# The second half's norm in five steps between the next sub-layer's weight tiles, and the old x fetched in two parts

## The chip, the cores and the metric

The kernel runs on 1 core of one Trainium2 chip. Its time is the device time of one execution in microseconds (us); the median of several executions counts, and lower is better. The engines of the core run side by side and wait for each other on semaphores: TensorE (PE for matmuls, PEld for their weight loads), VectorE (DVE), ScalarE (ACT), GpSimd (POOL) and the queue SP, which issues most of the DMAs. Each engine takes its instructions in the order in which they stand in its program.

## The reference, cut to what matters

The reference is one inference step through two layers of a decoder, for 512 prompt tokens and 64 sample tokens (8 sequences of 8) together, with a model width of 1024 and everything in float32. Each layer has three sub-layers: a SwiGLU feed-forward network (FFN), a token mixer (layer 0: a Mamba-2 state-space mixer, layer 1: sliding-window attention), and another FFN.

```python
for i in range(DEPTH):                                   # 2 layers
    mod = (cs @ ada_w[i] + ada_b[i]).reshape(bsz, 1, N_SUB, 3, D_MODEL)
    hin = modulated_norm(x, norm_pre[i, 0], mod[:, :, 0])
    f = swiglu(hin, ffn_w_in[i, 0], ffn_w_out[i, 0])
    x = x + FFN_RES * mod[:, :, 0, 2] * rms_norm(f, norm_post[i, 0])
    hin = modulated_norm(x, norm_pre[i, 1], mod[:, :, 1])
    o, ... = mixer(hin, ...)
    x = x + mod[:, :, 1, 2] * rms_norm(o, norm_post[i, 1])
    hin = modulated_norm(x, norm_pre[i, 2], mod[:, :, 2])
    f = swiglu(hin, ffn_w_in[i, 1], ffn_w_out[i, 1])
    x = x + FFN_RES * mod[:, :, 2, 2] * rms_norm(f, norm_post[i, 2])
```

Here `modulated_norm(x, g, m)` is `rms_norm(x, g) * (1 + m[:, :, 1]) + m[:, :, 0]`, and `swiglu` is `(silu(g) * u) @ w_out` with `g, u` the two halves of `h @ w_in`. Between two sub-layers, then, x gets the normed and gated output f of the one before, and a second norm of the new x makes the next input, hin.

## The kernel before

**Layout.** All activations are held with the model width on the 128 partitions, in 8 tiles (index k or o), and the 576 tokens along the free dimension. The tokens are worked on in two parts, which this document calls halves: half 0 is 256 prompt tokens, half 1 the other 256 prompt tokens and the 64 sample tokens (320 columns). Every weight and activation is split into a high part and a low part, so a product of a 128x128 weight tile is three matmuls (low weight x high activation, high x low, high x high), and a tile of 128 outputs over 1024 inputs is 8 x 3 = 24 matmuls per half. `load_w` fetches a weight tile by DMA into `raw` (two buffers), ScalarE casts the high part (L469, `whi` or, where extra buffers are borrowed, `wx`), and VectorE subtracts it to get the low part (L472).

**A boundary between sub-layers** is an object of `Boundary`. There are six; the last one writes the output. The five others go like this:

1. The last weights of the sub-layer are loaded in `run_out`. Before them, `open` fetches the old x from the DRAM copy `x_dram` in three DMAs (L94): x[0] (half 0, 1 MB), x[1] (the prompt tokens of half 1, 1 MB) and x[2] (the sample tokens, 256 KB).
2. `stat` gathers, for each output tile, the squares of f and, for half 0 on GpSimd (L335), the product of the old x[0] with f; for half 1 the products with x[1] and x[2] are matmuls (`gram`, L343).
3. `sums` turns them into two scales per token. They are broadcast over the partitions by matmuls into `rb` (L255): b1 for f, b2 for the new x.
4. `update(h)` adds the scaled f to x (L414, L415) and writes the normed `hin` of that half (L436 on VectorE, L438 on ScalarE, L439 on VectorE), two k at a time; for half 1 it does the sample tokens first (L407, L409, then L445 to L449). `update(0)` runs while `run_out` still works on half 1.
5. The next sub-layer begins in `run_in`: it takes the weights that `run_out` has already begun to load, loads the rest of the first 8 (an FFN) or 6 (a mixer), calls `update(1)`, and then does all these weight tiles on half 0 and after that all of them on half 1.

**What consumes the first weight tiles.** Each product goes to one of 4 PSUM buffers `g` (L501), and its `use` function frees that buffer. In an FFN the tiles alternate: a gate tile is read by ScalarE (`silu`, L724, into one of 3 `sil` buffers), an up tile by VectorE (L729, which frees the PSUM buffer), ScalarE (L730) and VectorE (L731, which frees the `sil` buffer). In the state-space mixer the first tile gives the time steps (L1100, ScalarE), and the next five are convolutions: a copy out of PSUM (L849, ScalarE, 2 buffers `xpt`), a first tap on ScalarE (L860), three taps on VectorE for half 0 (L863), a tanh (L869) and a last product (L870, VectorE); `acc`, which two of these share, has 2 buffers. After all six, `dt_path` computes the decays in one chain, mostly on VectorE. In attention the first six tiles are only copied out by ScalarE.

**What sets the order on an engine.** The program text gives priorities, not an order: a scheduler runs the program through a model of the chip and lets each engine take, among the instructions that are ready in the model's time, the one that stands first in the text. The order so found is fixed in the program. A few orders are pinned by hand with `behind`: `place(1, base)` puts the matmuls of the sums and of the two broadcasts of half 1 (`PL[1] = (25, 52, 64)`) behind the 26th, 53rd and 65th matmul of the next sub-layer.

Of the kernel before, what the change touches and what calls it, by code (L numbers as in the profile page):

```python
# [58 lines left out]
def body(ctx: ExitStack, tc: tile.TileContext, A, O):  # L59
# [28 lines left out]

    XO = ((0, 2048), (2048, 2048), (4096, 512))

    def x_copy(d, x, store):
        for t, (o, n) in zip(x, XO):
            a, b = d[:, o:o + n], t.rearrange("p k n -> p (k n)")
            nc.sync.dma_start(a if store else b, b if store else a)  # L94

    x = x_alloc()
# [39 lines left out]
    x_dram = dram.tile([128, 8 * T], F32, name="x_dram")  # L136
# [159 lines left out]
    class Boundary:  # L296
# [5 lines left out]
            self.end = (l, s) == (1, 2)  # L302
            self.marks = [{}, {}]

        def open(self):
            l, s = self.l, self.s
            state["xp_cm"] = tc.tile_pool(name=f"xpool{l}{s}", bufs=1, side="right", reuse_waits="tile")
            state["xp"] = state["xp_cm"].__enter__()
            x_cur[:] = x_alloc()
            x_copy(x_dram if l or s else A["xT"], x_cur, False)  # L310
            self.cms = [tc.tile_pool(name=f"{n}{l}{s}", bufs=1, side="right", reuse_waits="tile") for n in ("upd", "stats")]
            self.pool, pool = (cm.__enter__() for cm in self.cms)
            self.spool = pool
            mod_gate(l, s, self.mv)
            self.ns = 1 if self.end else 2
            self.gram = [None, None]
            self.acc = [pool.tile([128, 3 - h, n], F32, tag=f"st{h}", name=f"st{h}") for h, (_, n) in enumerate(HALF)]
            if not self.end:
                self.nmv = mod_vecs(*((l, s + 1) if s < 2 else (l + 1, 0)))
# [75 lines left out]
            self.cms.pop().__exit__(None, None, None)  # L395

        def update(self, h):
            f, b1 = self.f, self.b1
            if not self.end:
                b2 = self.b2  # L400
                if h == 0:
                    self.hin = hin_alloc()
            if self.end:
                return self.finish(h)
            if h == 1:
                ts = self.pool.tile([128, 8, 64], F32, tag="ts", name="ts", bufs=1)
                V.tensor_tensor(out=ts, in0=f[1][:, :, 256:320], in1=b1[:, 256:320].unsqueeze(1).to_broadcast([128, 8, 64]),  # L407
                                op=ALU.mult)
                V.tensor_tensor(out=x_cur[2], in0=x_cur[2], in1=ts, op=ALU.add)  # L409
                if not self.end:  # L410
                    norm_sample(self.pool, self.nmv, b2, self.hin)
            for kk in range(0, 8, 2):
                fs, xs = f[h][:, kk:kk + 2, 0:256], x_cur[h][:, kk:kk + 2, :]
                V.tensor_tensor(out=fs, in0=fs, in1=b1[:, 0:256].unsqueeze(1).to_broadcast([128, 2, 256]), op=ALU.mult)  # L414
                V.tensor_tensor(out=xs, in0=xs, in1=fs, op=ALU.add)  # L415
                if not self.end:
                    norm_prompt(self.pool, self.nmv, b2, self.hin, h, (kk, kk + 1))

        def finish(self, h):

# [60 lines left out]
    def gemm(w, acts, n, w0=0):  # L481

        return gemms([w], acts, n, w0)[0]
# [21 lines left out]
    def hin_acts(hin, h):  # L505
        return [(hin[h][:, 0, k, :], hin[h][:, 1, k, :]) for k in range(8)]
# [10 lines left out]
    def run_in(hin, items, first, ex, pend, between=None, pre=()):  # L517

        bd = last.pop() if first and last else None
        base = len(mms)  # L520
        ws = [bd.nextw[i] if bd and i < len(bd.nextw) else pre[i][0] if i < len(pre) else
              load_w(src, 1024, ex if i >= WR else None)
              for i, (src, _) in enumerate(items[:first])]
        if bd:
            bd.update(1)
            bd.close()
        for h in (0, 1):
            if between and h:
                between()
            for i, (w, (_, use)) in enumerate(zip(ws, items)):  # L530
                if h == 0 and i < len(pre):
                    use(h, gemm_part(w, hin_acts(hin, h), HALF[h][1], range(4, 8), pre[i][1]))
                else:
                    use(h, gemm(w, hin_acts(hin, h), HALF[h][1]))
            if bd and h == 0:
                bd.place(1, base)
        for src, use in items[first:]:
            w = load_w(src, 1024)
            for h in (0, 1):
                use(h, gemm(w, hin_acts(hin, h), HALF[h][1]))  # L540
            pend.step()
# [11 lines left out]
    def run_out(loads, acts, f, first, bd=None, r=0, ex=None, bias=None):  # L553


        def one(w, w0, o, h):
            t0, n = HALF[h]
            p = gemm(w, acts(h), n, w0)
            fs = f[h][:, o, :]
            if first:  # L560
                if bias is None:
                    S.copy(fs, p)
                else:
                    S.activation(out=fs, in_=p, func=AF.Identity, bias=bias[:, o:o + 1])
            else:
                V.tensor_tensor(out=fs, in0=p, in1=fs, op=ALU.add)  # L566
            if bd:
                bd.stat(o, h)

        nl = len(loads) - r  # L570
        for src, n, os_ in loads[:nl]:
            w = load_w(src, n)
            for o, w0 in os_:
                for h in (0, 1):
                    one(w, w0, o, h)
        if r:
            ws = [load_w(src, n, ex if i >= WR else None) for i, (src, n, _) in enumerate(loads[nl:])]
            todo = [(w, w0, o) for w, (_, _, os_) in zip(ws, loads[nl:]) for o, w0 in os_]
            for a in todo:
                one(*a, 0)  # L580
            base = len(mms)
            for a in todo[:B1]:
                one(*a, 1)
            bd.sums(0)
            for a in todo[B1:B2]:
                one(*a, 1)
            bd.update(0)
            for a in todo[B2:]:
                one(*a, 1)
            bd.place(0, base)  # L590
            bd.nextw = [load_w(src, 1024) for src in first_srcs(bd)]
            bd.sums(1)
            bd.close()
            if bd.end:
                bd.finish(1)
                bd.close()
            else:
                last.append(bd)
# [109 lines left out]
    def ffn(l, s, hin, f, pend, bd):  # L708
        si = 0 if s == 0 else 1
        sub = lambda name: tc.tile_pool(name=f"{name}{l}{s}", bufs=1, reuse_waits="tile")  # L710
        with sub("mid") as mp:
# [50 lines left out]
            pend.flush()  # L762
            ada_cm.__exit__(None, None, None)
            with sub("tail") as tp:
                bd.open()
                run_out(loads, halves(mids), f, False, bd, RF, borrow(tp, "wf", 2 * (RF - WR), mk * 128))


    def ssd(l, hin, f, pend, bd):
        with ExitStack() as cx:  # L770
# [336 lines left out]
            d, items = proj_items(0)  # L1107
# [57 lines left out]
            R2cm.__exit__(None, None, None)  # L1165
            Rcm.__exit__(None, None, None)
            with tc.tile_pool(name="ssdo", bufs=1, reuse_waits="tile") as ap[0]:
                bd.open()
                run_out(out_loads(3), yn_acts(yn), f, False, bd, 4)


# [514 lines left out]
```

## Time and profile before

| | |
|---|---|
| median of 3 runs | 2581.92 us (2581.41 to 2588.04) |
| the profiled execution | 2593.07 us, of which 2591.0 us from its first instruction to its last |
| mean granted TensorE clock | 0.977 of full |
| busy share: PE, PEld, DVE, ACT, POOL | 96%, 89%, 70%, 44%, 8% |
| DMA | 331 MB, 128 GB/s over the span |

The profiled execution lies 11.15 us above the median. Matmuls overlap each other, so the busy share of PE is not a share of its peak; what PE loses is seen in the gaps and in the granted clock, stretch by stretch. Matmul counts of a stretch include those that reach over its edges.

### The profile page before, as it was taken

To read this page: it belongs to the slowest core of one execution; us is meant where nothing else is said; L and a number is where in the kernel's file an instruction comes from. 1 tells how busy PE (TensorE), PEld (TensorE's weight loads), DVE (VectorE), ACT (ScalarE), POOL (GpSimd) and SP (SyncE) were. 2 spreads that over 40 slices of the span, in tenths; PEclk is the share of its full clock that TensorE was granted. 3 is DMA by queue.
4 is the path that set the end of the run, shared out by engine and by line. 5 is a ranking of instruction groups with operands and counts; after the bars stand their busy time and mean duration, and the time that the engine had idled before them with its cause. 6 is when DMAs were issued, how large, how long until landed. Compare 5 with 4: busy or idle time off the path is not lost.

```text
span 2591.0 us, 45688 instructions
## 1 busy us (share of the span) xinstructions
PE 2493.8 (96%) x18247; PEld 2309.2 (89%) x18247; DVE 1804.0 (70%) x3415; ACT 1152.3 (44%) x2396; POOL 202.8 (8%) x338
## 2 busy tenths in 40 slices
PE   6999999989999999999999999999999998999997
PEld 5999998877989878899999999999899788999997
DVE  5576766887768686667767757675766756577685
ACT  4343434554645454334424534342454664343343
POOL 1000000123131312000000100000010001000001
PEclk8999999999999999899999999999999998999998
DMA  7344534244444342344333343443436123233222
GB/s 261 106 167 135 191 134 167 94 117 130 122 131 107 131 115 107 120 138 127 122 135 120 121 139 107 167 177 126 168 124 202 34 70 107 94 101 103 91 94 110
DMA packets 119499, 331.04 MB, mean 128 GB/s; under 512 B 17903, under 2 KB 39903, under 8 KB 108671
## 3 DMA queue, kind: packets, MB, share of 16 engines
q1 hardware_dynamic: 100535, 245.46, 29.3%
q10 hardware_dynamic: 18752, 82.68, 9.3%
q8 instruction: 143, 2.34, 0.4%
q14 instruction: 69, 0.57, 0.1%
HBM read 301.63 MB, written 29.67 MB: 128 GB/s over the span
## 4 chain that ended last, share of the span: by engine, by line
PE 80%; DVE 8%; DMA 4%; ACT 3%; issue 3%; POOL 1%; SPq 0%; DVEq 0%; ACTq 0%; POOLq 0%
PE g L501 40%; PE g L673 29%; PE adaps L164 2%; DMA w<-scr_a 1%; PE gram L343 1%; DVE wlo L472 1%; DVE acc L863 1%; DMA raw<-in_w_out 1%; PE po L1298 1%; DVE hin L439 1%; PE py L947 1%; PE ssq L234 1%; DVE pn L436 1%; PE rb L255 1%; DMA x<-x_dram 1%
## 5 line engine op out<-in xcount | busy, mean ns | idle before, releaser
L501 PE MATMUL g<-hin,whi 128*128 128x320 f32 (+1 forms) x2528 | 533.4, 304 | 1.8 <-DVE hin L439 1.8
L501 PE MATMUL g<-mid,whi 128*128 128x320 f32 (+1 forms) x2432 | 489.3, 296 | 0.0
L673 PE MATMUL g<-hin,whi 128*128 128x288 f32 x2176 | 436.2, 294 | 0.0
L501 PEld LDWEIGHTS g<-hin,whi 128*128 128x128 f32 x2528 | 418.6, 194 | 10.3 <-issue 6.6
L501 PE MATMUL g<-hin,wlo 128*128 128x320 f32 (+1 forms) x1264 | 388.1, 309 | 16.1 <-ACT sil L724 7.0
L501 PEld LDWEIGHTS g<-mid,whi 128*128 128x128 f32 x2432 | 390.7, 188 | 1.1
L501 PE MATMUL g<-mid,wlo 128*128 128x256 f32 (+1 forms) x1216 | 359.8, 297 | 2.4 <-ACT mid L685 2.2
L673 PEld LDWEIGHTS g<-hin,whi 128*128 128x128 f32 x2176 | 349.1, 188 | 0.0
L673 PE MATMUL g<-tcmb,whi 128*128 128x288 f32 x1632 | 327.2, 294 | 0.0
L673 PE MATMUL g<-hin,wlo 128*128 128x288 f32 x1088 | 324.2, 298 | 0.0
L469 ACT CAST whi<-raw 128x1024 fp32r<-128x1024 f32 (+2 forms) x209 | 188.0, 900 | 236.3 <-PE g L501 162.5
L472 DVE TENSOR_TENSOR wlo<-raw,whi 128x1024 fp32r<-128x1024 f32 (+3 forms) x209 | 216.4, 1038 | 85.7 <-ACT whi L469 84.7
L501 PEld LDWEIGHTS g<-hin,wlo 128*128 128x128 f32 x1264 | 244.3, 194 | 33.7 <-issue 11.0
L673 PEld LDWEIGHTS g<-tcmb,whi 128*128 128x128 f32 x1632 | 262.5, 189 | 0.0
L673 PE MATMUL g<-tcmb,wlo 128*128 128x288 f32 x816 | 245.5, 301 | 0.0
L501 PEld LDWEIGHTS g<-mid,wlo 128*128 128x128 f32 x1216 | 228.6, 188 | 7.1 <-ACT mid L685 4.6
L652 ACT CAST whi<-scmb 128x512 fp32r<-128x512 f32 (+1 forms) x204 | 154.3, 760 | 160.8 <-PE g L673 83.5
L673 PEld LDWEIGHTS g<-hin,wlo 128*128 128x128 f32 x1088 | 204.1, 188 | 23.9 <-issue 23.9
L566 DVE TENSOR_TENSOR f<-g,f 128x256 f32<-128x256 f32 (+1 forms) x240 | 108.6, 455 | 143.4 <-PE g L501 142.2
L648 DVE TENSOR_TENSOR wlo<-scmb,whi 128x512 fp32r<-128x512 f32 (+1 forms) x204 | 175.6, 863 | 36.1 <-ACT whi L652 35.2
L673 PEld LDWEIGHTS g<-tcmb,wlo 128*128 128x128 f32 x816 | 153.3, 188 | 25.1 <-DVE ur L648 19.7
L652 ACT CAST whi<-raw 128x512 fp32r<-128x512 f32 x136 | 84.7, 623 | 166.2 <-PE g L673 98.4
(299 smaller groups left out, 3898.9 us busy)
## 6 DMA issues: line engine op xcount, KB each, us to landing
adaw<-in_ada_w ACTq DMA_DIRECT2D x56, 1024.0 KB, 5.4
raw<-in_w_in SPq DMA_DIRECT2D x108, 512.0 KB, 3.5
rawu<-in_w_in SPq DMA_DIRECT2D x68, 512.0 KB, 4.5
raw<-in_w_out SPq DMA_DIRECT2D x64, 384.0 KB, 3.1
raw<-in_w_out SPq DMA_DIRECT2D x64, 320.0 KB, 3.0
raw<-in_w_ssm SPq DMA_DIRECT2D x40, 512.0 KB, 3.5
x_dram<-x SPq DMA_DIRECT2D x10, 1024.0 KB, 3.9
x<-x_dram SPq DMA_DIRECT2D x10, 1024.0 KB, 6.3
```

The costliest lines, as they stand in the source:

```text
L164: PE.matmul(out=pt[32 * j:32 * j + 32, :w], lhsT=cs[:, k, :], rhs=aw[:, j * w:j * w + w], start=(k == 0), stop=(k == 7))
L234: ins = PE.matmul(out=ps[:, c0 + i:c0 + i + 1], lhsT=acc[:, o:o + 128], rhs=ones[:, 0:1], start=True, stop=True)
L255: ins = PE.matmul(out=r[:, c:e], lhsT=mul(y[:, i:i + 1], [128, 128]), rhs=ident[:, 128 - (e - c):128], start=True, stop=True)
L343: ins = PE.matmul(out=out, lhsT=a, rhs=b, start=(o == i == 0), stop=(o == 7), skip_group_check=True)
L436: V.scalar_tensor_tensor(out=tm, in0=x_cur[h][:, k, :], scalar=mv["gs"][:, k, 0:1], in1=r[:, :256], op0=ALU.mult, op1=ALU.mult)
L469: S.copy(hi[:, :n], raw[:, :n])
L472: i = (V if early and c < PSP else eng or V).tensor_tensor(out=lo[:, c:e], in0=raw[:, c:e], in1=hi[:, c:e].bitcast(F32), op=ALU.subtract)
L501: mms.append(PE.matmul(out=p[:, :n], lhsT=wt[:, a:b], rhs=at, start=(k == j == 0), stop=(j == 2 and k == K - 1)))
L566: V.tensor_tensor(out=fs, in0=p, in1=fs, op=ALU.add)
L648: e.tensor_tensor(out=out, in0=a, in1=b, op=op)
L652: S.copy(w[0][:, c:c + n], src)
L673: mms.append(PE.matmul(out=p, lhsT=wt[:, o], rhs=x, start=(first and k == j == 0), stop=(k == 3 and j == 2), skip_group_check=True))
```

## The change

`update` becomes a generator, `updates`, of five steps for half 1: the sample tokens, then k = 0 and 1, 2 and 3, 4 and 5, 6 and 7. `run_in` no longer does `update(1)` ahead of its products: it does one step after each of the first weight tiles on half 0 has been used, and closes the boundary's pool after the last of them. So a tile's `use` now stands in the text ahead of the steps that follow it. The instructions of the norm and of the `use` functions themselves are the same, and so are the pinned places.

Besides, `open(False)` fetches only x[0], in the four FFN sub-layers and in the state-space mixer; the DMAs of x[1] and x[2] stand in the text after the loads of the last weights in `run_out` (`bd.rest()`). Attention calls `open()` and keeps all three together.

```diff
-    def x_copy(d, x, store):
-        for t, (o, n) in zip(x, XO):
+    def x_copy(d, x, store, parts=(0, 1, 2)):
+        for t, (o, n) in ((x[i], XO[i]) for i in parts):
             a, b = d[:, o:o + n], t.rearrange("p k n -> p (k n)")
             nc.sync.dma_start(a if store else b, b if store else a)
...
+        def rest(self):
+
+            if self.more:
+                x_copy(*self.more, False, (1, 2))
+            self.more = None
+
-        def open(self):
+        def open(self, rest=True):
...
-            x_copy(x_dram if l or s else A["xT"], x_cur, False)
+            self.more = (x_dram if l or s else A["xT"], x_cur)
+            x_copy(*self.more, False, (0,))
+            if rest:
+                self.rest()
...
         def update(self, h):
+            for _ in self.updates(h):
+                pass
+
+        def updates(self, h):
...
                 if not self.end:
                     norm_sample(self.pool, self.nmv, b2, self.hin)
+                yield
             for kk in range(0, 8, 2):
...
                 if not self.end:
                     norm_prompt(self.pool, self.nmv, b2, self.hin, h, (kk, kk + 1))
+                yield
...
-        if bd:
-            bd.update(1)
-            bd.close()
+        steps = bd.updates(1) if bd else iter(())
         for h in (0, 1):
...
                     use(h, gemm(w, hin_acts(hin, h), HALF[h][1]))
+                next(steps, None)
             if bd and h == 0:
+                for _ in steps:
+                    pass
+                bd.close()
                 bd.place(1, base)
...
             ws = [load_w(src, n, ex if i >= WR else None) for i, (src, n, _) in enumerate(loads[nl:])]
+            bd.rest()
...
-                bd.open()
+                bd.open(False)
                 run_out(loads, halves(mids), f, False, bd, RF, borrow(tp, "wf", 2 * (RF - WR), mk * 128))
...
-                bd.open()
+                bd.open(False)
                 run_out(out_loads(3), yn_acts(yn), f, False, bd, 4)
```

## Rows read from the trace of the kernel before

**Rows 1.** The page, part 4: the chain that ended last, by engine.
```profile
PE 80%; DVE 8%; DMA 4%; ACT 3%; issue 3%; POOL 1%; SPq 0%; DVEq 0%; ACTq 0%; POOLq 0%
```

**Rows 2.** PE's timeline, starts of half 1 at three FFN entries.
```profile
1079.41 0.64 PE L501 MATMUL g<-hin,wlo 128*128 128x320 f32 x1 [3.26 <-ACT sil L724]
...
1508.80 2.97 PE L501 MATMUL g<-hin,wx 128*128 128x256 f32 x24
1515.47 0.63 PE L501 MATMUL g<-hin,wlo 128*128 128x320 f32 x1 [3.70 <-ACT sil L724]
...
2188.31 5.49 PE L501 MATMUL g<-hin,wx 128*128 128x256 f32 x24 [4.07 <-DVE sil L729]
```

**Rows 3.** Windows: length, busy of PE, PEld, DVE, ACT, POOL, PEclk, DMA, GB/s.
```profile
1515.00:1520.00 5.00, 4.53 (x17) 4.53 (x18) 2.71 (x8) 1.49 (x5) 0.00 (x0) 0.50 0.28 110
1520.00:1525.00 5.00, 5.00 (x31) 5.00 (x30) 1.23 (x1) 1.38 (x2) 0.00 (x0) 0.85 0.00 0
```

**Rows 4.** VectorE's timeline, second FFN entry shown (1492 to 1518 us).
```profile
1494.68 0.69 DVE L407 TENSOR_TENSOR ts<-f,rb 128x512 f32<-128x512 f32 x1 [0.71 <-PE rb L255]
...
1514.51 0.42 DVE L731 TENSOR_TENSOR mid<-sil,mid 128x256 fp32r<-128x256 f32 x1
1514.84 0.87 DVE L439 SCALAR_TENSOR_TENSOR hin<-pn,modraw,hin 128x256 fp32r<-128x256 f32 x2
1515.64 1.07 DVE L729 TENSOR_TENSOR sil<-g,sil 128x256 f32<-128x256 f32 x3
```

**Rows 5.** VectorE's timeline, first and third FFN entry (from 1076 and 2168 us).
```profile
1078.79 0.86 DVE L439 SCALAR_TENSOR_TENSOR hin<-pn,modraw,hin 128x256 fp32r<-128x256 f32 x2
...
2173.45 0.69 DVE L446 TENSOR_TENSOR pns<-pns,rb 128x512 f32<-128x512 f32 x1 [2.58 <-PE rb L255]
...
2188.18 0.86 DVE L439 SCALAR_TENSOR_TENSOR hin<-pn,modraw,hin 128x256 fp32r<-128x256 f32 x2
```

**Rows 6.** Windows (columns as in rows 3): matmuls that wait for hin, twice.
```profile
505.00:510.00 5.00, 3.20 (x15) 1.96 (x13) 4.52 (x12) 2.52 (x7) 0.10 (x1) 1.00 0.51 210
1043.00:1047.00 4.00, 1.78 (x8) 1.18 (x8) 4.00 (x10) 1.04 (x3) 0.00 (x0) 1.00 0.16 66
1048.00:1057.00 9.00, 8.60 (x41) 8.59 (x41) 3.48 (x8) 2.93 (x5) 2.74 (x7) 0.50 0.49 160
```

**Rows 7.** VectorE's timeline, entry of the state-space mixer (488 to 511 us).
```profile
490.87 0.51 DVE L863 SCALAR_TENSOR_TENSOR acc<-xpt,c_convw,acc 128x256 f32<-128x256 f32 x1 [1.97 <-ACT acc L860]
...
507.60 0.47 DVE L863 SCALAR_TENSOR_TENSOR acc<-xpt,c_convw,acc 128x256 f32<-128x256 f32 x1
```

**Rows 8.** PE's timeline, the longest stall on `xpt`, state-space entry.
```profile
523.42 9.24 PE L501 MATMUL g<-hin,wx 128*128 128x320 f32 x48 [2.58 <-ACT xpt L849]
```

**Rows 9.** Windows (columns as in rows 3): state-space entry, attention entry.
```profile
490.00:560.00 70.00, 59.81 (x400) 55.30 (x400) 62.77 (x130) 36.29 (x83) 17.76 (x39) 0.95 0.44 121
1930.00:1965.00 35.00, 35.00 (x272) 34.32 (x272) 30.95 (x60) 15.40 (x32) 3.24 (x7) 1.00 0.50 176
```

**Rows 10.** SP's timeline at the end of the first FFN.
```profile
421.22 8.52 SPq L467 DMA_DIRECT2D raw<-in_w_out  x4
429.78 2.19 SPq L94 DMA_DIRECT2D x<-in_xT  x3
433.47 1.71 SPq L467 DMA_DIRECT2D raw<-in_w_out  x2
```

**Rows 11.** PE's timeline there: the last weights of half 0.
```profile
436.27 4.47 PE L501 MATMUL g<-mid,wx 128*128 128x256 f32 x36
444.33 6.95 PE L501 MATMUL g<-mid,wx 128*128 128x256 f32 x36 [3.59 <-DVE wx L472]
```

**Rows 12.** The chain of waits there, in order of time.
```profile
429.78 5.80 DMA x<-in_xT
```

**Rows 13.** The page, part 6: DMA issues, KB each, us to landing.
```profile
raw<-in_w_in SPq DMA_DIRECT2D x108, 512.0 KB, 3.5
...
raw<-in_w_out SPq DMA_DIRECT2D x64, 384.0 KB, 3.1
```

More of the change, by code (lines that the diff above doesn't have):

```diff
@@ L403, in update @@
             if self.end:
-                return self.finish(h)
+                self.finish(h)
+                return
             if h == 1:
```

## The prediction

> **What bounds the kernel now.** I read the chain that ended last first: PE holds 80% of it [rows 1], so the time is PE's, and a change pays only where PE waits or runs at the lower clock. I then looked along PE's timeline for gaps, at the six boundaries above all, because that is where both edits work. Three things stand out.
>
> At each of the three FFN entries that follow a boundary, PE stops for 3.26, 3.70 and 4.07 us around the turn from half 0 to half 1, and what ends the wait is a `use`: the silu of a gate tile (L724) twice, the product of an up tile (L729) once [rows 2]. The reader is to see in VectorE's timeline why. The norm of half 1 starts with L407 at 1494.68, and nearly every `use` of an up tile stands behind it: three L729 in a row come only at 1515.64, behind the last L439 [rows 4]. With up tiles unread, PSUM and `sil` buffers stay taken, and PE has nowhere to write. After the stop the granted clock is 0.50 in a window with 17 matmuls in 4.53 us of PE's time, and 0.85 in the next [rows 3]; 0.85 of 5 us is 1.5 us more at half clock, so some 6.0 us from 1515.47 run at 1.2 instead of 2.4 GHz.
>
> At the entry of the state-space mixer VectorE is the busy one, 62.77 of 70 us [rows 9]; PE waits there first for hin and later for `xpt` (2.58 us in its longest stall) [rows 6, 8]. At the attention entry PE is busy for all of 35 us at clock 1.00 [rows 9], so nothing is to be had.
>
> At the end of the first FFN PE stops for 3.59 us before the last two weight tiles of half 0, and those 36 matmuls then take 6.95 us where the 36 before took 4.47 [rows 11]. The other three FFN ends have the same stop, of 2.68 to 3.39 us. The fetch of x[0], 5.80 us, lies on the chain just before [rows 12].
>
> **The norm in steps: an FFN entry.** No instruction is added or removed; 30 VectorE instructions of the norm and the L729 and L731 of the up tiles change places. In the new text tile 1 (up) stands ahead of the second step and tile 3 (up) ahead of the fourth; tiles 5 and 7 stand behind all five. In the old order tile 1's L731 (1514.51) already ran ahead of the last L439 (1514.84) [rows 4], so only tile 3 puts something new ahead of the norm's end: one L729 and one L731, 1.07/3 = 0.36 us each [rows 4], 0.7 us together. In return tiles 1 and 3 free their PSUM and `sil` buffers early, and PE can go on until it lacks hin. What is late next is therefore the last pair of hin: PE needs it for the last 6 of the 24 matmuls of the first tile of half 1. A half-0 tile takes 2.97 us [rows 2], so by columns (320 for 256) I estimate a half-1 tile at 3.6 us and six matmuls at 0.9.
>
> - Second entry shown. Lost before: the stop of 3.70, and the clock: 6.0 us / 0.267 = 22 matmuls, each 4.53/17 - 3.6/24 = 0.117 us slower, 2.6 us. Together 6.3. After: half 0 ends at 1508.80 + 2.97 = 1511.77, an unhindered first tile would end 3.6 later at 1515.4; the last hin comes at 1514.84 + 0.87 + 0.7 = 1516.4, and with 0.9 the tile ends at 1517.3 [rows 2, 4]. Lost after: 1.9. Gain 4.4.
> - First entry, in the same way: 3.26 + 2.6 (taken over, since it restarts at the same place) = 5.9 before; last hin 1078.79 + 0.86 + 0.7, tile end 1081.3, against 1076.15 + 3.6 = 1079.8: 1.5 after [rows 2, 5]. Gain 4.4.
> - Third entry: here the stop falls before the last tile of half 0, whose 24 matmuls take 5.49 instead of 2.97 us [rows 2]: 4.07 + 2.5 = 6.6. VectorE sits idle for 2.58 us before L446 at 2173.45 [rows 5]; tile 1's two instructions fit into that. Last hin 2188.18 + 0.86 + 0.7 + 0.9 = 2190.6, unhindered end 2184.24 + 2.97 + 3.6 = 2190.8: nothing lost after. Gain 6.6.
>
> Together 15.4 us. Each has two ends: nothing, if the wait for hin takes the whole place of the old one, and all of what was lost (5.9, 6.3, 6.6, in sum 18.8). I stay with the worked values, because they follow instruction by instruction from the old order. The cover that this needs is that PE's first 18 matmuls of half 1 find their hin. A wait is added too: L729 of tile 3 waits for PE, with the fourth and fifth step queued behind it on VectorE and half 1 waiting for those. Where the fixed order puts it too early, that is at most one tile, 2.97 us [rows 2], per entry.
>
> **The norm in steps: the state-space entry.** Here each `use` costs VectorE four instructions (three L863, one L870), and tiles 1 to 4 stand ahead of the last step; of the first tile one L863 ran before the norm anyway, and its next came only at 507.60 [rows 7]. So up to 15 instructions of 0.47 us, 7 us, move ahead of the last hin, and half 1 with the time-step chain behind it starts that much later. In return the convolutions no longer pile up: the stall of 2.58 us [rows 8] and its like are theirs. VectorE's idle time between 490 and 560 us is 70 - 62.77 = 7.2 us [rows 9], and no more than that can be won while it is the bound. Between -7 and +7.2 I take 0. The attention entry, whose `use` functions need no VectorE and which has no gap, gets 0 too.
>
> **x in two parts.** The text of the old kernel has the three x DMAs ahead of all eight weight loads, and yet SP issued six of those first, then the three x, then the last two [rows 10]. The queue goes by readiness, then. x[1] and x[2] were issued by 429.78 + 2.19 = 431.97, and the next weight load not before 433.47, since its buffer has to be freed by VectorE. Moving x[1] and x[2] behind it in the text does not make that buffer free sooner; they should leave at the same moment as before, and the edit costs and gives nothing. If they did leave last, they would be covered: half 1 begins no sooner than 444.33 + 6.95 = 451.3 [rows 11]. What that would give: a 512 KB load lands in 3.5 us and one of 384 KB in 3.1 [rows 13], so 0.4 per 128 KB, and 1 MB alone at 3.5 + 1.6 = 5.1 against 5.80 [rows 12]: 0.7 us at each of four FFN ends, 2.8 us at the low end; at the high end the whole stop with its clock, 3.59 + 2.48 = 6.1 [rows 11], 24 us for four. The Trainium skill (DMA: Bandwidth & Descriptors, section on queues, rings and completion order) says that each DMA engine consumes the descriptors of one ring in ring order. By that rule x[1] and x[2], which stand behind x[0], never held it up, and the gain would be 0 even if they moved; the trace before has no x[0] fetched alone to show it.
>
> **The sum.** 15.4 + 0 + 0. The profiled execution took 2593.07 us, so it would take 2577.7; the median of the runs shown is 11.15 us lower, and the same gain taken from 2581.92 gives 2566.5.
>
> **Rivals.**
> - The clock falls all the same. Matmuls that dribble as hin arrives kept clock 1.00 from 505 to 510 us, with 3.20 us of PE busy in 5, but after 1043 to 1047, with 1.78 in 4, nine us ran at 0.50 [rows 6]. I expect 3.6 us of work in about 5, nearer the first. If it falls at all three entries, 2.6 each goes back: 2566.5 + 7.8 = 2574. The Trainium skill (TensorE: Matmul & The Clock Gate, "Loop structure matters more than you think") speaks for this rival: it calls a wait in front of every matmul the loop that goes cold.
> - x[1] and x[2] do leave behind the last weights: 2.8 to 24 us more, 2542 to 2564. Against it stands the order that SP shows [rows 10].
> - Slower, through the state-space entry: if each of tiles 1 to 4 holds the norm not for its instructions alone but for its whole way over ScalarE as well, it is 1.97 + 4 x 0.47 = 3.9 us per tile [rows 7], 15.5 for four, and a clock fall of 2.6 on top: 18 us late, and the decay chain with it. That is 2 to 3 us more than the FFN entries bring: 2585. It decides from 15.4 us; beyond 23 the kernel is slower by more than 0.3%. For it: VectorE is nearly full there. Against: the same convolutions are then out of the way later.
> - The scheduler's order hardly changes. It takes what is ready in the model's time; if the model sees the up tiles ready late, the norm still goes first: 2582. Against: tile 1's L729 and half of its work already slip ahead.
>
> **How the numbers follow.** A difference within 0.3% (7.7 us) can hardly be told from none here. Forecast 0.45 (own range 2559 to 2574), clock 0.17, x 0.12, state-space 0.14, no new order 0.12. The forecast, x and half of the clock case are faster, 0.66; the rest of the clock, no new order and nearly half of the state-space case are the same, 0.25; 0.09 slower. The range reaches from forecast plus the 7.2 of the state-space entry and part of the x case (2555) to the state-space rival's 2585.
>
> **What would show it.** Right: L729 of tile 3 ahead of the last L439 at the FFN entries; PE's stops of 3.26, 3.70 and 4.07 gone, with short ones on hin instead, at clock 1.00; SP with x, x, x before the last two weight loads, and the 3.59 us stop of the first FFN's end still there. Wrong: a window at 0.50 after those entries; a stop before half 1 at the state-space entry well above 7 us; x[1] issued after the last w_out load.

## The result, and the profile after

The changed kernel takes 2559.75 us (median of 6 executions, 2557.07 to 2561.28); the kernel before took 2587.35 us beside it (2581.41 to 2591.27). The ratio is 0.9894, with a 95% interval of 0.9879 to 0.991: 27.6 us less, where 15.4 were forecast. The profiled execution took 2559.38 us, with a span of 2557.2 us and a mean granted clock of 0.984 (before 2591.0 and 0.977).

The chain that ended last is still PE's (page, part 4, shares by engine; before [rows 1]):
```profile
PE 81%; DVE 8%; DMA 4%; ACT 4%; issue 2%; POOL 1%; SPq 0%; DVEq 0%; ACTq 0%; POOLq 0%
```

**The FFN entries.** PE's timeline after, at the first and second entry, answers [rows 2]. The lines of the kernel have shifted: L501 is now L517, the gate's silu L743, the up product L748, the last step of hin L455.
```profile
1075.18 0.42 PE L517 MATMUL g<-hin,wlo 128*128 128x320 f32 x1 [1.22 <-ACT hin L454]
...
1502.42 0.56 PE L517 MATMUL g<-hin,whi 128*128 128x320 f32 x2 [0.17 <-DVE hin L455]
```
The stops of 3.26, 3.70 and 4.07 us are gone. What is left waits for hin, 1.22 and 0.17 us, and at the third entry nothing. VectorE's timeline at the second entry answers [rows 4]:
```profile
1495.86 0.41 DVE L748 TENSOR_TENSOR sil<-g,sil 128x256 f32<-128x256 f32 x1
...
1503.47 0.41 DVE L748 TENSOR_TENSOR sil<-g,sil 128x256 f32<-128x256 f32 x1
1503.80 0.87 DVE L455 SCALAR_TENSOR_TENSOR hin<-pn,modraw,hin 128x256 fp32r<-128x256 f32 x2
```
The reader is to see two up products ahead of the last L455, where before three in a row came behind it (in both kernels one more, tile 1's, runs ahead of the whole norm). The first 10 us of half 1 at the three entries, in windows (columns as in [rows 3]: length, busy of PE, PEld, DVE, ACT, POOL, clock, DMA, GB/s):
```profile
1071.00:1081.00 10.00, 8.78 (x60) 8.51 (x59) 8.80 (x20) 4.74 (x11) 0.00 (x0) 1.00 0.27 107
1500.04:1510.04 10.00, 9.83 (x68) 9.56 (x67) 8.34 (x17) 5.31 (x10) 0.00 (x0) 1.00 0.31 114
2164.20:2174.20 10.00, 10.00 (x71) 10.00 (x70) 8.27 (x18) 5.21 (x10) 0.00 (x0) 1.00 0.26 107
```
The clock is 1.00 in all of them; [rows 3] had 0.50 and 0.85 at the second entry.

**The FFN ends.** SP's timeline at the end of the first FFN answers [rows 10]:
```profile
420.28 8.65 SPq L483 DMA_DIRECT2D raw<-in_w_out  x4
428.97 0.43 SPq L94 DMA_DIRECT2D x<-in_xT  x1
432.65 1.70 SPq L483 DMA_DIRECT2D raw<-in_w_out  x2
434.40 0.90 SPq L94 DMA_DIRECT2D x<-in_xT  x2
```
x[1] and x[2] leave behind the last two weight loads, and so they do at all four FFN ends. The DMA view gives what that does to the landing (issues in a window, KB each, median us to landing). Before, in the window that holds the last two weight loads:
```profile
raw<-in_w_out SPq DMA_DIRECT2D x2, 384.0 KB, 6.1
```
After, x[0] with the weight loads just before it, and then the first of the last two loads:
```profile
x<-in_xT SPq DMA_DIRECT2D x1, 1024.0 KB, 5.8
...
raw<-in_w_out SPq DMA_DIRECT2D x1, 384.0 KB, 3.9
```
x[0] lands no sooner than before (5.8 us, [rows 12] had 5.80). The weights do: 3.9 us instead of 6.1 here, and over the four FFN ends each of the two loads takes 3.5 to 5.0 us where it took 5.6 to 7.2.

PE's timeline there, against [rows 11]:
```profile
435.81 8.70 PE L517 MATMUL g<-mid,wx 128*128 128x256 f32 x69
...
449.18 0.31 PE L517 MATMUL g<-mid,wlo 128*128 128x320 f32 x1
451.64 0.97 PE L352 MATMUL gram<-f,x 128*128 128x128 f32 x6 [2.15 <-ACT f L337]
```
and the windows behind it:
```profile
448.00:452.00 4.00, 1.85 (x14) 1.59 (x13) 2.63 (x4) 2.76 (x6) 0.74 (x1) 1.00 0.00 0
452.00:456.00 4.00, 4.00 (x24) 3.81 (x23) 1.85 (x4) 2.60 (x8) 0.47 (x1) 0.66 0.41 131
456.00:460.00 4.00, 4.00 (x17) 3.81 (x16) 0.82 (x1) 0.35 (x1) 2.45 (x7) 0.50 0.36 131
460.00:464.00 4.00, 4.00 (x30) 3.89 (x30) 2.72 (x6) 2.33 (x5) 0.00 (x0) 0.98 0.02 4
```
The stop of 3.59 us is gone and half 0 runs through at full clock. But a new stop of 2.15 us stands in front of the gram matmuls, and the clock falls behind that one. The second and third FFN end have the same new stop (2.08 and 2.13 us).

**Where the time went.** Stretches of PE's timeline, in us. Each kernel was profiled twice (the second profiles are the last two runs below).

| stretch | before | after |
|---|---|---|
| first FFN entry, from its first matmul on hin to the first on the combined tiles | 116.8, 116.3 | 112.5, 112.9 |
| second FFN entry, the same | 107.6, 105.9 | 101.4, 101.4 |
| third FFN entry, the same | 115.1, 114.4 | 107.4, 106.0 |
| three FFN ends in sum, from the last matmul on the combined tiles until half 1 begins | 84.4, 85.4 | 67.5, 67.5 |
| the same ends, until the first gram matmul | 101.0, 102.3 | 89.3, 89.4 |
| the same ends, until the next sub-layer's first matmul | 177.7, 180.5 | 172.2, 170.7 |
| last FFN end, until PE's last instruction | 54.4, 54.5 | 50.2, 50.1 |

By the means, the entries gain 17.3 us (3.8, 5.4 and 8.1; 18.3 in the first pair of profiles, 16.3 in the second), the three FFN ends 7.6 and the last one 4.3. The three ends are 17.4 us ahead when half 1 begins, 12.3 at the gram matmuls and 7.6 at the next sub-layer: more than half is given back on the way. At the end of the state-space mixer the stop in front of gram goes from 2.41 to 1.19 us. At the state-space entry VectorE is busy for 67.67 of the 70 us that [rows 9] had with 62.77; the entry starts 1.8 us earlier in this profile, so the window holds a little more of it:
```profile
490.00:560.00 70.00, 64.20 (x448) 60.71 (x447) 67.67 (x142) 37.74 (x89) 29.99 (x40) 0.98 0.45 132
```

### The profile page after: what moved, and what is told of

It is laid out like the page before. It is cut to its first block, busy times and chain, and to the rows that moved or that the text cites. A ratio compares the mean times of both kernels' runs of the same rounds, so it can differ in the third digit from the quotient of the medians.

```text
span 2557.2 us, 45699 instructions
## 1 busy us (share of the span) xinstructions
PE 2479.4 (97%) x18247; PEld 2295.0 (90%) x18247; DVE 1804.4 (71%) x3415; ACT 1152.8 (45%) x2396; POOL 218.1 (9%) x338
## 4 chain that ended last, share of the span: by engine, by line
PE 81%; DVE 8%; DMA 4%; ACT 4%; issue 2%; POOL 1%; SPq 0%; DVEq 0%; ACTq 0%; POOLq 0%
PE g L517 41%; PE g L692 29%; PE adaps L164 2%; DMA w<-scr_a 1%; PE gram L352 1%; DVE wlo L488 1%; DVE acc L882 1%; DMA raw<-in_w_out 1%; DMA raw<-in_w_in 1%; PE py L966 1%; DVE st L358 1%; DMA adaf<-in_ada_w 1%; POOL stt L344 1%; PE ssq L234 1%; PE po L1317 1%
## 5 line engine op out<-in xcount | busy, mean ns | idle before, releaser
L517 PE MATMUL g<-hin,whi 128*128 128x320 f32 (+1 forms) x2528 | 525.8, 302 | 0.7 <-DVE hin L455 0.6
L517 PE MATMUL g<-mid,whi 128*128 128x320 f32 (+1 forms) x2432 | 491.6, 297 | 0.0
L517 PEld LDWEIGHTS g<-hin,whi 128*128 128x128 f32 x2528 | 413.8, 192 | 9.1 <-issue 6.6
L517 PEld LDWEIGHTS g<-mid,whi 128*128 128x128 f32 x2432 | 392.9, 189 | 1.1
L517 PE MATMUL g<-hin,wlo 128*128 128x320 f32 (+1 forms) x1264 | 383.7, 307 | 10.1 <-ACT hin L454 4.2
L517 PE MATMUL g<-mid,wlo 128*128 128x256 f32 (+1 forms) x1216 | 361.6, 299 | 2.3 <-ACT mid L704 2.2
L517 PEld LDWEIGHTS g<-hin,wlo 128*128 128x128 f32 x1264 | 241.5, 192 | 27.2 <-issue 11.5
L517 PEld LDWEIGHTS g<-mid,wlo 128*128 128x128 f32 x1216 | 229.9, 190 | 6.9 <-ACT mid L704 4.4
L584 DVE TENSOR_TENSOR f<-g,f 128x256 f32<-128x256 f32 (+1 forms) x240 | 108.3, 454 | 135.0 <-PE g L517 133.8
```

What stands on the lines that cost most here:

```text
L517: mms.append(PE.matmul(out=p[:, :n], lhsT=wt[:, a:b], rhs=at, start=(k == j == 0), stop=(j == 2 and k == K - 1)))
```

## The experiments

Each ratio is to the kernel before, run on the same chip; us are the ratio's distance from 1 times the median of before there (for the change, the difference of the two medians).

| run | ratio, 95% interval | us | three FFN ends in sum, us |
|---|---|---|---|
| the change | 0.9894, 0.9879 to 0.991 | -27.6 | 172.2, 170.7 |
| steps only | 0.9929, 0.9911 to 0.9948 | -18.4 | 179.3 |
| split only | 0.9953, 0.9936 to 0.9969 | -12.2 | 175.4 |
| FFN entries only | 0.9898, 0.9878 to 0.9919 | -26.4 | 172.3 |
| add one tile late | 0.983, 0.9809 to 0.9851 | -44.0 | 158.7 |
| old kernel, add late | 0.998, 0.9967 to 0.9994 | -5.2 | 171.0 |
| one fetch, casts early | 0.991, 0.9889 to 0.993 | -23.3 | 173.4 |
| two fetches, casts late | 0.9884, 0.987 to 0.9899 | -30.0 | 172.8 |
| tiles one by one | 0.9909, 0.9893 to 0.9925 | -23.5 | 170.9 |

The last column is read as in the table above, up to the next sub-layer's first matmul; before has 177.7 and 180.5 there. It is one execution each, and those of before differ by 2.8 us, so differences of that size in it show nothing.

### The two halves of the change

Steps only:
```diff
-                bd.open(False)
+                bd.open()
...
-            bd.rest()
```


> The norm in steps stays, x is fetched as before in one call of three parts. My theory now: the steps bring what the two traces show at the three FFN entries (4.3 + 6.3 + 7.7 = 18.3 us) and next to nothing at the state-space entry, so 17 to 20 us less than before, ratio 0.9925 to 0.9935, and the stop of 3.59 us at the end of the first FFN is still there. Rival A (the prediction's terms, x worth nothing): the steps bring all of the 27.6 us, ratio about 0.989. Rival B: the entries gained only because the boundary ahead of them ended sooner, so the steps alone bring less than 10 us, ratio above 0.996.

Measured 0.9929: as the theory said. Rival A (the prediction's own sum, with x at nothing) and rival B fall. PE's timeline of this run shows the old stop, still there and with a slow clock behind it (18 matmuls in 3.92 us):
```profile
445.34 3.92 PE L517 MATMUL g<-mid,wx 128*128 128x256 f32 x18 [3.61 <-DVE wx L488]
```

Split only:
```diff
-        steps = bd.updates(1) if bd else iter(())
+        if bd:
+            bd.update(1)
+            bd.close()
+        steps = iter(())
...
             if bd and h == 0:
-                for _ in steps:
-                    pass
-                bd.close()
                 bd.place(1, base)
```


> x is fetched in two parts, the norm of half 1 stays one piece ahead of the next sub-layer's weights. My theory now: the two parts bring about 10 us (at the four FFN ends 0.9 + 2.7 + 1.9 + 4.3 and 1.6 at the state-space end, as the two traces show), ratio 0.995 to 0.997, with the stops of 3.3 to 4.1 us at the FFN entries as before. Rival A (the prediction's step): nothing, ratio 0.999 to 1.001. Rival B: what the end of each FFN wins up to the start of half 1 (21 us in sum) is all kept, because the new stop in front of the gram matmuls belongs to the steps, ratio about 0.992.

Measured 0.9953, as the theory said. The prediction's step, nothing from x, is outside the interval, and so is the 0.992 of rival B. PE's timeline has the new stop in front of gram without the steps, and the old stop at the first FFN entry:
```profile
449.75 1.52 PE L352 MATMUL gram<-f,x 128*128 128x128 f32 x5 [2.15 <-ACT f L337]
...
1077.06 0.41 PE L517 MATMUL g<-hin,wlo 128*128 128x320 f32 x1 [3.28 <-ACT sil L743]
```
So the stop in front of gram comes with the split alone. The two halves add up: 18.4 + 12.2 = 30.6 against 27.6, within the intervals.

### The state-space entry

```diff
-        steps = bd.updates(1) if bd else iter(())
+        if bd and bd.s == 0 and not bd.l:
+            bd.update(1)
+            bd.close()
+            steps = None
+        else:
+            steps = bd.updates(1) if bd else iter(())
```
(and behind each tile a step is taken only where there are steps)

> As after, but at the state-space entry the norm of half 1 is one piece ahead of the weights as before. My theory now: that entry is worth 1 to 2 us either way, so the ratio stays at 0.989 to 0.990. Rival A: the steps help there by up to the 7.2 us that VectorE was idle, ratio 0.992. Rival B: the steps cost there and the gain came from elsewhere in the stretch, ratio below 0.988.

Measured 0.9898 against 0.9894: the steps at this entry are worth nothing that can be measured. Rival A's 0.992 lies just outside the interval, and of rival B's values (below 0.988) only its very edge is left. The median is 2561.7 us, 2 us from that of the change.

### What eats the gain at the FFN ends

VectorE's timeline of the changed kernel shows what the new stop is made of. L584 takes a finished tile into `f`, L358 sums the tile's statistics and waits for GpSimd's product:
```profile
445.99 0.96 DVE L358 TENSOR_TENSOR st<-st,stt 128x768 f32<-128x768 f32 x1 [0.63 <-POOL stt L344]
446.86 0.42 DVE L584 TENSOR_TENSOR f<-g,f 128x256 f32<-128x256 f32 x1
449.19 0.96 DVE L358 TENSOR_TENSOR st<-st,stt 128x768 f32<-128x768 f32 x1 [1.91 <-POOL stt L344]
450.06 0.48 DVE L584 TENSOR_TENSOR f<-g,f 128x320 f32<-128x320 f32 x1
```
Half 1 begins on PE at 444.34, but half 0's last tile is taken only at 446.86, and the first tile of half 1 only at 450.06, 3.2 us later, since the sum of the tile before stands ahead of it and waits. The gram matmuls need that first tile. In the kernel before the same two accumulates (there L566) lie as far apart, but PE, held up by the stop for the weights, starts gram only at 456.56 and waits 0.30 us:
```profile
451.77 0.42 DVE L566 TENSOR_TENSOR f<-g,f 128x256 f32<-128x256 f32 x1
...
454.98 0.48 DVE L566 TENSOR_TENSOR f<-g,f 128x320 f32<-128x320 f32 x1
```
The edit puts the sum of each tile of half 0 behind the next tile's accumulate, as an order on VectorE:
```diff
+        def flush(self):
+            if self.late:
+                out, b = self.late
+                i = V.tensor_tensor(out=out, in0=out, in1=b, op=ALU.add)
+                if self.fi:
+                    behind(i, self.fi)
+            self.late = None
...
-                V.tensor_tensor(out=self.acc[h][:, :ns], in0=self.acc[h][:, :ns], in1=st[:, :ns, :n], op=ALU.add)
+                self.late = (self.acc[h][:, :ns], st[:, :ns, :n])
...
-                V.tensor_tensor(out=fs, in0=p, in1=fs, op=ALU.add)
+                i = V.tensor_tensor(out=fs, in0=p, in1=fs, op=ALU.add)
+                if bd:
+                    bd.fi = i
```
(`flush` is called at the start of `stat` and of `sums`; `stt` has three buffers)

> As after, and in half 0 of every FFN end the sum of the norm's statistics on VectorE (st <- st, stt) is placed behind the next tile's accumulate, with a third stt buffer. No instruction is added or removed. My theory now: the new stop of 2.1 us in front of the gram matmuls at three FFN ends comes from VectorE taking tile 7's accumulate only behind the sums of tiles 5 and 6, and half 1's first accumulate only behind the sum of tile 7, each of which waits for GpSimd's product (3.2 us a tile). With the order turned round the stop shrinks to under 0.5 us and the window at 0.50 behind it goes, so 6 to 11 us less than after: ratio 0.985 to 0.987. Rival A: the stop is bounded by ScalarE's three activations a tile, not by that order: no change from after, 0.989 to 0.990. Rival B: the stop goes but returns at the sums of half 0, ratio 0.988 to 0.990.

Measured 0.983: 44 us less than before, 16 less than the change, and more than the 6 to 11 expected. It beats both kernels. VectorE's timeline of this run (L599 accumulates, L335 sums):
```profile
445.07 0.42 DVE L599 TENSOR_TENSOR f<-g,f 128x256 f32<-128x256 f32 x1
445.80 0.96 DVE L335 TENSOR_TENSOR st<-st,stt 128x768 f32<-128x768 f32 x1 [0.31 <-POOL stt L355]
446.68 0.42 DVE L599 TENSOR_TENSOR f<-g,f 128x256 f32<-128x256 f32 x1
447.39 0.96 DVE L335 TENSOR_TENSOR st<-st,stt 128x768 f32<-128x768 f32 x1 [0.30 <-POOL stt L355]
448.80 0.49 DVE L599 TENSOR_TENSOR f<-g,f 128x320 f32<-128x320 f32 x1 [0.45 <-PE g L532]
```
The pace is 1.6 us a tile, and the first tile of half 1 waits for PE alone. The windows behind it stay at clock 1.00:
```profile
452.00:456.00 4.00, 4.00 (x32) 3.93 (x33) 2.21 (x5) 2.56 (x7) 1.59 (x3) 1.00 0.44 139
456.00:460.00 4.00, 4.00 (x31) 3.81 (x30) 2.85 (x7) 2.00 (x4) 1.87 (x5) 1.00 0.34 123
```
The three ends take 158.7 us, 12.7 less than the mean of the change, and nothing is given back between gram and the next sub-layer (76.0 us, against 82.8 and 81.3 in the change and 76.6 and 78.2 before). Where the rest of the 16 us lies was not found, and the third buffer was not tried without the new order.

The same edit on the old kernel:

> The kernel before, with only the sum of the statistics placed one tile later at the FFN ends (the edit of the run before that had it on top of the change). Theory: in the old kernel the same pace of 3.2 us a tile on VectorE lies under the stop for the weights and the slow matmuls behind it, and cost 0.30 us in front of the gram matmuls; so the edit alone is worth 0 to 3 us, ratio 0.999 to 1.000. Rival: it is worth its 16 us by itself, ratio 0.994; then the change and this edit are independent and the stop in front of the gram matmuls was not a consequence of the change.

Measured 0.998, 5.2 us: above the 0 to 3 expected (the interval, 1.6 to 8.5 us, reaches into it), far from the rival's 16. The stop for the weights is still there:
```profile
440.65 4.57 PE L516 MATMUL g<-mid,wx 128*128 128x256 f32 x36 [3.50 <-DVE wx L487]
```
The 36 matmuls behind it took 4.57 us where [rows 11] have 6.95: in this execution the clock did not fall there. It is also 5.7 us faster than the median of this run, so how much of the 5.2 us is the clock, and why it did not fall, stays open.

### Transfers or ScalarE's order?

The split changed two things at the FFN ends: when the last weights land, and, in each engine's written order, where ScalarE casts them: ahead of the statistics of tile 3 instead of behind those of tile 4. Two runs cross these; in their edits c6 and c7 are those two casts, and bd.acts[0, o] holds ScalarE's three statistics instructions of tile o in half 0. Steps and one fetch, with the casts forced early:
```diff
             for a in todo:
                 one(*a, 0)
+            if r == 8 and not bd.end:
+                behind(bd.acts[0, 3][0], c6)
+                behind(bd.acts[0, 3][2], c7)
```


> The steps, x in one call (x[1] and x[2] ahead of the last two weight loads), but on ScalarE the casts of those two weights are placed where they stand after the change: ahead of the statistics of tile 3 of half 0, instead of behind those of tile 4. Theory, two parts: the two loads land 6.1 us after issue behind x (3.9 and 3.5 without it), about 439.6 us in the run's time, and the old order then held the cast until 441.5. With the place alone the stop of 3.6 us shrinks to 1.5 to 2.5; ratio between that of the steps alone (0.993) and that of the change (0.989), about 0.991. Rival A, only ScalarE's order matters: 0.989. Rival B, only the landing matters: 0.993 or more, since ScalarE now stands waiting and holds the statistics.

Measured 0.991, as the theory said, but the interval (0.9889 to 0.993) holds the values of both rivals as well, so the time does not decide; the trace does. ScalarE's timeline shows it standing for the weights, which land 6.1 us after issue:
```profile
438.39 0.83 ACT L489 CAST wx<-raw 128x768 fp32r<-128x768 f32 x1 [3.08 <-DMA raw<-in_w_out]
```
PE's stop for them is 1.38 us at each of the three ends, not 3.6.

The change whole, with the casts forced late (`behind(c6, bd.acts[0, 4][2])`, `behind(c7, bd.acts[0, 5][1])`):

> The change whole, with x[1] and x[2] behind the last two weight loads, but on ScalarE the casts of these weights are put back where they stood before: behind the statistics of tile 4 and the first two instructions of tile 5. Theory: the loads land at 436 to 437 as after the change, and it does not help, since their casts come at 441 again: the stop of 3 to 3.6 us at the FFN ends is back, ratio 0.992 to 0.994, as with the steps alone. Rival, the order of the transfers alone decides: 0.989 to 0.990, and no stop.

Here the theory's time was wrong: 0.9884, no slower than the change. Its mechanism was seen all the same, with stops of 3.21, 3.03 and 2.71 us:
```profile
442.03 2.42 PE L521 MATMUL g<-mid,wx 128*128 128x256 f32 x18 [3.21 <-DVE wx L492]
```
But no stop in front of gram follows (0.12 to 0.14 us). The clock stays up behind the first of these stops and falls behind the other two, in the first 4 us to 0.50 and 0.60:
```profile
448.00:452.00 4.00, 4.00 (x29) 3.98 (x28) 3.01 (x5) 3.05 (x6) 0.90 (x2) 1.00 0.00 0
452.00:456.00 4.00, 3.87 (x29) 3.39 (x28) 1.92 (x4) 2.63 (x6) 0.18 (x1) 1.00 0.43 131
...
1434.39:1438.39 4.00, 4.00 (x18) 4.00 (x19) 2.11 (x3) 1.97 (x4) 0.73 (x1) 0.50 0.41 134
1877.58:1881.58 4.00, 4.00 (x21) 4.00 (x22) 2.19 (x4) 1.97 (x4) 0.73 (x1) 0.60 0.37 131
```
So the three ends come to 173.4 (casts early), 172.8 (weights landing early) and 172.2 and 170.7 (both), against 179.3 with neither. Either alone gives what both give, as far as these profiles tell. With both, gram begins 7.5 us sooner in sum than with the casts late (89.3 against 96.8 us into the ends), but from there to the next sub-layer it takes 82.8 us against 76.0: what is won ahead of gram goes to the stop there and to the clock behind it. What the split has over the early casts is the rest: the last FFN end (50.2 us against 53.1) and the end of the state-space mixer (a stop of 1.19 us in front of gram against 2.44).

### The order of the first tiles on PE

In the changed kernel's instruction order PE takes the first two tiles of half 1 at the FFN entries in turns: a dozen or more matmuls of the first, then pieces of both. Before, they stood one by one, and PE's timeline shows one matmul with `wlo` and two with `whi` for each k; in turns, those of two tiles come together (second entry, after):
```profile
1502.82 0.30 PE L517 MATMUL g<-hin,wlo 128*128 128x320 f32 x1
1502.96 0.75 PE L517 MATMUL g<-hin,whi 128*128 128x320 f32 x4
```
The edit restores the old order:
```diff
+                    m0 = len(mms)
                     use(h, gemm(w, hin_acts(hin, h), HALF[h][1]))
+                    if bd and h and i and bd.s:
+                        behind(mms[m0], mms[m0 - 1])
```


> The change whole, but at the FFN entries the tiles of half 1 are put one behind the other on PE, as they stood before; after the change the first two tiles are interleaved there (12 to 13 matmuls of the first, then pieces of both by turns). Theory: the prediction counted 1.5 and 1.9 us of waiting for the last hin at the first and second entry and 0 at the third, and the interleaving is what saved these, and the clock with them: 3 to 6 us more than after, ratio 0.990 to 0.992, with waits of 0.5 to 2 us for hin in the first tile. Rival: hin comes in time anyway and the order of the tiles is worth nothing, ratio 0.989.

Measured 0.9909, within what the theory said, though the interval (from 0.9893) reaches down to the change's 0.9894. The windows decide it (first 10 us of half 1 at the three entries, as above for the change):
```profile
1066.55:1076.55 10.00, 8.34 (x44) 7.32 (x43) 7.99 (x18) 3.89 (x8) 0.00 (x0) 0.83 0.26 107
1499.73:1509.73 10.00, 9.07 (x58) 8.15 (x57) 7.76 (x17) 4.62 (x9) 0.00 (x0) 1.00 0.31 115
2163.20:2173.20 10.00, 8.62 (x54) 7.64 (x53) 7.77 (x17) 4.19 (x9) 0.00 (x0) 1.00 0.27 106
```
PE does 44, 58 and 54 matmuls in that time, where the change does 60, 68 and 71 (60 to 68, 66 to 71 and 71 in the seven profiles with steps and without this edit). That is 43 fewer, 6.1 us at 0.141 us each (10.00/71), and at the first entry the clock falls to 0.83 again. The entries' stretches are 4.7 us longer in sum than the mean of the change's two profiles.

### Both kernels profiled again

> The kernel before, unchanged, profiled a second time, to see how far the granted clock behind a stop repeats. If it is set by the program alone, the three FFN ends take 59.9, 58.8 and 59.7 us again (within 0.3) from the last matmul on the combined tiles to the first one of the next sub-layer, and the 36 matmuls behind the stop of 3.59 us take 6.95 again. If it differs from execution to execution, as the run with the sums placed late on the old kernel suggests (36 matmuls in 4.57 us behind a stop of 3.50), the ends differ by 1 to 3 us with the stops unchanged.

> The changed kernel, unchanged, profiled a second time. If the clock is set by the program alone, the FFN ends take 59.0, 56.5 and 57.8 us again and the windows behind the stop of 2.15 us show 0.66 and 0.50 at the first end. If it differs from execution to execution, the three ends come out in another order, with the stops of 2.1 us unchanged.

The kernel before took 59.1, 59.0 and 62.4 us at the three ends (59.1, 58.8 and 59.7 in the first profile), the changed one 56.7, 56.2 and 57.8 (58.3, 56.1 and 57.8). The 59.9, 59.0 and 56.5 in the two expectations run to a later matmul than the first of the next sub-layer. In the kernel before the stop for the weights at the third end went from 3.25 to 4.07 us. The new stops of the changed kernel repeat to 0.1 us (2.15, 2.17, 2.10). The clock behind them does not: 0.83 and 0.74 in the second profile, in the windows that had 0.66 and 0.50.
```profile
452.00:456.00 4.00, 4.00 (x26) 3.81 (x27) 1.96 (x5) 2.58 (x8) 0.91 (x1) 0.83 0.41 131
456.00:460.00 4.00, 4.00 (x24) 3.81 (x23) 1.26 (x2) 0.45 (x1) 2.55 (x7) 0.74 0.39 131
```
In the kernel before the 36 matmuls behind the first stop took 6.95 us again. A difference of 1 to 3 us at one end, in one profile, is therefore no evidence. The sums over three ends repeat to 2.8 and 1.5 us, and the ratios rest on four to twelve executions each.

## Why the prediction was right, and where it was wrong

- **The norm in steps, FFN entries: right in its mechanism, a little low in its terms.** Up products went ahead of the last hin (tile 5's too, where the prediction had only tile 3's), the three stops went, and the clock stayed up. Forecast 4.4, 4.4 and 6.6, in sum 15.4 us; measured 18.4 by the steps alone, and 3.8, 5.4 and 8.1, in sum 17.3, by the two pairs of profiles. At the second entry the term that was off is "lost after": 1.9 us forecast, a wait of 0.17 measured (at the first entry 1.5 and 1.22). The prediction kept the old order of PE, where a tile must be finished before the next begins. In the new one PE works on the second tile meanwhile, and putting the tiles one by one again brought a loss back, with one at the third entry too. At the third entry the gain exceeds all that the prediction had as lost there; where the other 1.5 us come from was not traced.
- **The state-space entry at 0: right.** It had a range of -7 to +7.2; leaving the steps out there changed the ratio from 0.9894 to 0.9898, within the intervals.
- **The attention entry at 0: right.** From its first matmul to the start of half 1 it takes 20.8 us in both profiles of either kernel.
- **x in two parts: wrong, and this is the step that failed.** That x[1] and x[2] "should leave at the same moment as before" does not hold. SP issues its DMAs in the order that the program fixes: x[1] and x[2] now stand behind two loads that leave at 432.65, 3.3 us after x[0] has been issued, and they leave after them, at 434.40. The prediction read the order of before as one of readiness at run time ("The queue goes by readiness, then") and took it to survive a move in the text. Why the scheduler's model put them there is in no trace.
- **Its price, put at nothing, was looked for in the wrong transfer.** The prediction asked whether x[0] would land sooner. It does not (5.8 us both times), and here the trace agrees with the rule of the Trainium skill that the prediction named, that a DMA engine consumes the descriptors of one ring in ring order (DMA: Bandwidth & Descriptors, section on queues, rings and completion order). But the same rule, applied to what stands behind x instead of ahead of it, speaks of the weights: they land 3.9 us after issue instead of 6.1. The forecast of 0 left this term out. Split alone: 12.2 us, where the forecast had 0 and the rival 2.8 to 24.
- **The rivals.** "x[1] and x[2] do leave behind the last weights" (chance 0.12, 2542 to 2564) is what happened, together with the forecast's gain at the entries. "The clock falls all the same" did not happen at the entries, where all windows show 1.00; it happened behind gram at the FFN ends, where the prediction had no stop. The Trainium skill (TensorE: Matmul & The Clock Gate, "Loop structure matters more than you think"), named for this rival, says of a loop with a long DMA wait between every matmul that PE goes cold in it. Neither place here is that loop: at the entries waits for hin of 1.22 and 0.17 us left 1.00, and behind gram one stop of 2.15 us, ended by ScalarE and not by a DMA, was followed by 0.66 and 0.50. "Slower, through the state-space entry" and "The scheduler's order hardly changes" did not happen.
- **The number.** 2559.75 us is inside the range (2555 to 2585), 6.8 under the forecast. The gain is counted from 2587.35, the median beside it, and not from the 2581.92 that the forecast started with; taken from there, the same 27.6 us would give 2554.3, just below the range, so that the time lies inside it is in part luck. The gain is 12.2 us more than forecast. That this equals the 12.2 of the split alone is luck too: the steps brought 3.0 more than forecast, and the two together 3.0 less than their sum.
- **Where the rest of the gain at the FFN ends went.** At the three ends half 1 comes forward by 17.4 us in sum, and 7.6 are kept. Shown: a new wait, VectorE's sums of statistics ahead of the next tile's accumulate, in front of gram, and the clock behind it; with the sums one tile later both are gone, and the kernel takes 2544.37 us.

## What to carry to other kernels

When transfers are moved on a queue, ask who stands behind them, not only when they land themselves. When a stop is taken away, find the engine that was slow under its cover: here VectorE's pace of 3.2 us a tile had lain under the stop for the weights, and one sum placed a tile later gave 16 us on top, where the split had given 12. And read a wait against PE's new instruction order, not the old one: two tiles taken in turns hide a late operand that one tile in sequence would wait for.

## What the runs showed of the hardware

The granted clock does not follow the length of a stop alone. In one execution of the old kernel with the sums late, PE's stops for the weights at the three FFN ends were 3.50, 3.06 and 3.11 us, with the same matmuls behind each. The first 4 us behind them:
```profile
440.65:444.65 4.00, 4.00 (x33) 4.00 (x34) 2.64 (x3) 1.18 (x4) 0.53 (x1) 1.00 0.69 215
1439.92:1443.92 4.00, 4.00 (x18) 4.00 (x19) 1.35 (x1) 0.21 (x1) 0.53 (x1) 0.50 0.64 213
1887.96:1891.96 4.00, 4.00 (x33) 4.00 (x34) 2.65 (x3) 1.17 (x4) 0.54 (x1) 1.00 0.66 181
```
The clock fell to half behind the shortest of the three and stayed up behind the longer two. With the casts late it stayed at 1.00 behind 3.21 us and fell to 0.50 behind 3.03. Behind 2.15 us in front of gram the windows show 0.66 and 0.50, and in a second execution of the same program 0.83 and 0.74. What decides between these was not settled.

The last two weight loads of an FFN end (384 KB each) land later with more ahead of them on the queue: 5.6 to 7.2 us after issue behind x[0], x[1] and x[2], 3.5 to 5.0 us behind x[0] alone.
